# Where the high and low weight buffers of a decoder step lie in SBUF: low ones first, four small tiles between

## The chip, the cores and the metric

The kernel runs on one core of a Trainium2 chip. It is one launch. The metric is the time of the device for that launch, in microseconds, as the median over repeated runs; lower is better. One further execution is taken with the hardware profiler, and its page and trace are what is read below.

## The reference, cut to what matters

The kernel computes one layer of a hybrid decoder for 512 prompt tokens and 8 × 8 sample tokens, which share the weights (576 columns in all). Everything is float32. The places with large matrix products, which the change touches, are these:

```python
def hybrid_layer(x, mem_k, mem_v, ...):
    proj = (_rms(x) * g_pre_mix) @ w_in            # 1024 -> 5,656 columns
    z, xbc, dt_raw, q, k, v, ig, fg, og = jnp.split(proj, split_at, axis=-1)
    ...
    mix = jnp.concatenate([y_ssd, h_ml], axis=-1) @ w_out   # 2048 -> 1024
    x = x + _rms(mix) * g_post_mix
    qx = (_rms(x) * g_pre_x) @ w_xq                # 1024 -> 1024
    ...
    o = attention(qx, mem_k, mem_v) @ w_xo         # 1024 -> 1024
    x = x + _rms(o) * g_post_x
    u = _rms(x) * g_pre_ffn
    f = (jax.nn.silu(u @ w_gate) * (u @ w_up)) @ w_down     # 1024 -> 2816 -> 1024
    return x + _rms(f) * g_post_ffn, ...

mk, mv = memory_kv(mem_prompt, g_mem, w_mem_k, w_mem_v)     # two products of 256 memory rows, 1024 -> 1024
```

The convolution, the two recurrences (SSD and mLSTM, chunk by chunk) and the attention over the memory are left out here; none of them reads the buffers that move.

## The kernel before, in words

**Split products.** Activations lie with their features on the 128 partitions and their tokens along the free dimension. Each float32 operand is split in two: a high part, which is the value as the type of TensorE's fast float32 keeps it (F32R), and a low part, the rest. A product is three matmuls, summed in PSUM: high weights by high input, high weights by low input, low weights by high input. `gemm` (L195) issues such a triple for each of the 128-row blocks of the contraction, eight for an input of 1024: L202, L203 and L205. A weight tile of 128 × 1024 holds the eight 128 × 128 blocks that make 128 output features. The stationary operand of each matmul is one such block, the moving operand a run of 256, 288, 320 or 512 columns of the input. In the cross-attention output and the feed-forward the sums go by a scheme of seven products in place of eight (class `Seven`, `mul` L1846 to L1848), with the same triple over 288 columns.

**The weight buffers.** All weights come from HBM in float32 and are split on the chip. `split_w` (L172) does it for the input projection, the values, the output projection, the queries and the memory's products: SP loads into a tile `raw`, ScalarE copies it to `whi` with rounding (L180), and VectorE subtracts the two into `wlo` (L187; part of the columns on GpSimd in some tiles). Where `acc` is set, the second half of `wlo` is made in another way: ScalarE writes the negated high part (L184) and a DMA on GpSimd's queue adds the weights from HBM to it (L185). `whi` and `wlo` are each a tag with three buffers in the pool `weights`, `raw` one with two. `weights` (L1147) keeps the last three pairs by name for a second use. `cast` (L1546) and, in the feed-forward, `high1`, `parts2` and `place3` (L1794 to L1817) take buffers of the same two tags. There are other weight tiles that lie elsewhere: a second set of `whi` and `wlo` in a pool of the cross-attention, `wacc` for low parts of the feed-forward, `wmh` and `wml` for the memory's first products, `wdh` and `wdl` for the first down projections, `u3h`, `u3l` and `w3`.

**Where they lie.** A pool places a tag when its first tile is asked for, one behind the other, all buffers of a tag together. The line that asks first is L306: two pairs, `whi` then `wlo`. So the pool begins with three `whi` of 4096 bytes a partition, then three `wlo`, then the two `raw`. The pool `const` lies ahead of it.

**The small tiles.** At the end of each RMS norm over the features the reciprocal root of a token's sum of squares is made as a column. For four of these norms `root_step` (L1586) does the last Newton step on VectorE, with three short instructions, into a tile `r` of three floats a partition; `root_rows` (L1594) transposes its columns into rows on TensorE. The four tiles (`px0_r`, `p30_r`, `px1_r`, `p31_r`) are asked for in `root_step`, each with a name of its own, from the pool `const`.

**Order.** The order of the instructions on each engine is set by the scheduler at build time from a simulated timeline, under the constraints that the kernel gives with `issue_after` and, in the later stages, a plan written out as a list of positions (`at_`, L1537). Loads of weights stand on SP's queue, the adding DMAs on GpSimd's. Neither addresses nor offsets enter that order unless a buffer is shared.

Of the kernel before, what the change touches and what calls it, by code (L numbers as in the profile page):

```python
# [11 lines left out]
F32 = mybir.dt.float32  # L12
F32R = mybir.dt.float32r
# [6 lines left out]
P = 128  # L20
# [95 lines left out]
def build(nc, tc, ctx, I, O):  # L116
# [3 lines left out]
    cp = ctx.enter_context(tc.tile_pool(name="const", bufs=1))  # L120
    wp = ctx.enter_context(tc.tile_pool(name="weights", bufs=1))
# [181 lines left out]
        mm(psw[:, 0:256], wz[:, 0:128], wz, start=True, stop=True, skip_group_check=True)  # L303
    S.dma_start(par, I["par"])

    wi = [[wp.tile([P, 1024], F32R, name=k, tag=k, bufs=3) for k in ("whi", "wlo")] for _ in range(2)]  # L306
    raws = [wp.tile([P, 1024], F32, name="raw", tag="raw", bufs=2) for _ in range(2)]
    for k in range(KT):
        if k % 2 == 0:
# [24 lines left out]
    for k in range(KT):  # L334
        for (hi, lo), pss in zip(wi, ps0):
            wh, wl = hi[:, k * P:(k + 1) * P], lo[:, k * P:(k + 1) * P]
# [373 lines left out]
    for g in range(2):  # L710
# [13 lines left out]
        for h in range(8):  # L724
            k, j = h % 2, (8 * g + h) // 2
# [163 lines left out]
    for h in range(4):  # L889
        q, k = qk[:, h, :], qk[:, 4 + h, :]  # L890
# [78 lines left out]
    for hb in range(2):  # L969
        r = slice(32 * hb, 32 * hb + 32)  # L970
# [614 lines left out]

    def root_step(name):  # L1586
        v, y, a = R[name]
        r = cp.tile([P, 3], F32, name=name + "_r")
        V.tensor_tensor(a, y, y, op=ALU.mult)
        V.scalar_tensor_tensor(a, a, -0.5, v, op0=ALU.mult, op1=ALU.mult)  # L1590
        V.scalar_tensor_tensor(r, a, 1.5, y, op0=ALU.add, op1=ALU.mult)
        R[name] = r
# [11 lines left out]
    def norm(name, ssq, i, out, alloc, p, d):  # L1604

        at_(p, root_sums, name, ssq, i, alloc)
        at_(p + 0.4, root_step, name)
        at_(d, root_rows, name, i, alloc)
        at_(d + 0.2, root_copy, name, i, out)
# [744 lines left out]
```

## Time and profile before

| | |
|---|---|
| median of 3 timed runs | 1088.65 us (1088.47 to 1088.78) |
| profiled execution, its own time | 1087.01 us |
| its span | 1085.2 us |
| granted TensorE clock, mean | 0.998 |

The page gives the busy time of each engine, the span in 40 slices, the chain of work that ended last, and groups of instructions by line, engine, operation and tiles. PE is TensorE's matmuls, PEld its loading of weights, DVE is VectorE, ACT ScalarE, POOL GpSimd, and SP the engine that issues loads. A group `L205 PE MATMUL ps_in<-uh,wlo 128*128 128x256 f32 x272` has its line, its engine and operation, the PSUM tile it writes, the moving tile and the stationary one, their shapes and the count; behind the bar stand the busy time in us, the mean of one in ns, and the engine's idle time ahead of them with what ended most of it. In the matmuls in order of time each row begins with the start in us and the duration in us, rounded to 0.01.

Matmuls overlap: one takes some 300 ns from its start to its end, and starts while two others are still running. So for TensorE the distance between starts is the time that a matmul costs, and it is worked out from the first and last row of an unbroken run and the number of steps between.

### The profile page before, as it was taken

The page shows a single profiled execution, that of the slowest core. Times are in us where ns is not written, and L with a number is a line of the kernel's source. Part 1 is how long each engine was busy: PE and PEld are TensorE (multiplying, and loading weights), DVE is VectorE, ACT ScalarE, POOL GpSimd, SP SyncE. Part 2 cuts the span into 40 slices and gives each one's busy share as a digit, 9 for nine tenths or more (in the row PEclk, how much of TensorE's full clock was granted, in tenths as well). Part 3 has the DMA queues.
Part 4 walks back from the last instruction along what each step waited for, and adds up shares of the span by engine and source line. Part 5 has one row for each costly group of instructions (what it writes and reads, how often), then busy time and mean ns, then how long its engine had stood idle before and what let it go on. Part 6 is the DMA issues. An engine that isn't in the chain of part 4 may idle for free.

```text
span 1085.2 us, 20708 instructions
## 1 busy us (share of the span) xinstructions
PE 1075.0 (99%) x8124; PEld 1022.1 (94%) x8124; DVE 752.4 (69%) x1507; ACT 610.9 (56%) x1098; POOL 228.0 (21%) x305
## 2 busy tenths in 40 slices
PE   9999999999999999999999999999999999999997
PEld 9999887778999999999999989999999999999997
DVE  6896785658877775568755546766467887787556
ACT  7867632355654555656555545645566566656653
POOL 1332643313113111000154301100011111111000
PEclk9999999999999999999999999999999999999999
DMA  6775535435654449653458775643486697578532
GB/s 211 179 159 126 161 111 172 165 80 185 190 152 144 110 123 324 226 193 101 152 194 288 271 252 180 239 133 92 135 176 137 159 203 163 117 189 184 125 131 88
DMA packets 58966, 182.29 MB, mean 168 GB/s; under 512 B 6604, under 2 KB 11852, under 8 KB 58356
## 3 DMA queue, kind: packets, MB, share of 16 engines
q1 hardware_dynamic: 42740, 138.06, 38.6%
q0 software_dynamic: 15552, 41.95, 19.6%
q8 instruction: 64, 1.05, 0.4%
q10 hardware_dynamic: 576, 0.95, 0.3%
q14 instruction: 34, 0.28, 0.1%
HBM read 160.28 MB, written 20.65 MB: 167 GB/s over the span
## 4 chain that ended last, share of the span: by engine, by line
PE 86%; DVE 5%; ACT 4%; issue 2%; DMA 2%; POOL 0%; DVEq 0%; SPq 0%; ACTq 0%; POOLq 0%
PE ps_in L203 4%; PE ps_in L202 4%; PE ps_in L205 4%; PE ps_v L815 3%; PE ps_o L205 3%; PE ps_o L203 3%; PE ps_g L1846 3%; PE ps_g L1847 3%; PE ps_o L202 3%; PE ps_u L1847 3%; PE ps_u L1848 3%; PE ps_u L1846 3%; PE ps_g L1848 3%; PE ps_dn L1846 2%; PE ps_dn L1847 2%
## 5 line engine op out<-in xcount | busy, mean ns | idle before, releaser
L202 PE MATMUL ps_in<-uh,whi 128*128 128x320 f32 (+1 forms) x544 | 162.9, 300 | 0.5 <-DVE cb L451 0.5
L205 PE MATMUL ps_in<-uh,wlo 128*128 128x320 f32 (+1 forms) x544 | 162.3, 299 | 0.3 <-DMA wlo<-win 0.3
L203 PE MATMUL ps_in<-ul,whi 128*128 128x320 f32 (+1 forms) x544 | 161.8, 298 | 0.0
L180 ACT CAST whi<-raw 128x1024 fp32r<-128x1024 f32 (+1 forms) x104 | 105.2, 1013 | 100.0 <-PE ps_in L203 25.9
L187 DVE TENSOR_TENSOR wlo<-raw,whi 128x512 fp32r<-128x512 f32 (+1 forms) x96 | 93.7, 978 | 75.1 <-ACT whi L180 74.0
L202 PEld LDWEIGHTS ps_in<-uh,whi 128*128 128x128 f32 x544 | 102.8, 189 | 3.3 <-issue 1.7
L205 PEld LDWEIGHTS ps_in<-uh,wlo 128*128 128x128 f32 x544 | 102.3, 188 | 1.5 <-DMA wlo<-win 0.5
L203 PEld LDWEIGHTS ps_in<-ul,whi 128*128 128x128 f32 x544 | 102.4, 188 | 0.6
L185 POOL DMA_DIRECT2D wlo<-win x32 | 27.8, 869 | 80.7 <-ACT wlo L184 70.0
L1847 PE MATMUL ps_g<-b,whi 128*128 128x288 f32 x144 | 42.5, 295 | 0.0
L1846 PE MATMUL ps_g<-b,whi 128*128 128x288 f32 x144 | 42.4, 295 | 0.0
L1847 PE MATMUL ps_u<-b,whi 128*128 128x288 f32 x144 | 42.4, 295 | 0.0
L1846 PE MATMUL ps_u<-b,whi 128*128 128x288 f32 x144 | 42.2, 294 | 0.0
L1819 ACT CAST whi<-rawx 128x1024 fp32r<-128x1024 f32 (+1 forms) x26 | 25.6, 984 | 27.9 <-PE ps_dn L1847 13.8
L192 DVE TENSOR_TENSOR wlo<-sw,whi 128x1024 fp32r<-128x1024 f32 (+1 forms) x26 | 29.6, 1140 | 14.9 <-ACT whi L191 14.8
L202 PE MATMUL ps_xo<-qh,whi 128*128 128x288 f32 x128 | 38.5, 303 | 0.2 <-ACT whi L180 0.2
L205 PE MATMUL ps_o<-mixm_h,wlo 128*128 128x256 f32 (+1 forms) x128 | 37.9, 296 | 0.0
L1798 ACT CAST whi<-raw 128x1024 fp32r<-128x1024 f32 (+1 forms) x26 | 25.6, 983 | 21.8 <-PE ps_g L1847 9.7
L203 PE MATMUL ps_xo<-ql,whi 128*128 128x288 f32 x128 | 37.8, 296 | 0.0
L205 PE MATMUL ps_o<-mixs_h,wlo 128*128 128x320 f32 (+1 forms) x128 | 37.7, 295 | 0.0
L203 PE MATMUL ps_o<-mixs_l,whi 128*128 128x320 f32 (+1 forms) x128 | 37.7, 295 | 0.0
L203 PE MATMUL ps_o<-mixm_l,whi 128*128 128x256 f32 (+1 forms) x128 | 37.7, 295 | 0.0
(769 smaller groups left out, 3853.6 us busy)
## 6 DMA issues: line engine op xcount, KB each, us to landing
raw<-win SPq DMA_DIRECT2D x35, 512.0 KB, 4.0
raw<-wout SPq DMA_DIRECT2D x17, 512.0 KB, 3.7
raw<-wxq SPq DMA_DIRECT2D x13, 512.0 KB, 6.0
raw<-wgate SPq DMA_DIRECT2D x13, 512.0 KB, 3.6
raw<-wup SPq DMA_DIRECT2D x13, 512.0 KB, 5.1
wlo<-win POOLq DMA_DIRECT2D x24, 256.0 KB, 5.1
kva<-vc SPq DMA_DIRECT2D x11, 512.0 KB, 5.0
raw<-wv SPq DMA_DIRECT2D x10, 512.0 KB, 4.0
```

Of the source, the lines that this page charges most:

```text
L180: casts.append(A.copy(hi[:, :n], raw[:, :n]))
L185: G.dma_start(lo[:, a:b], src[:, a:b], accum_op=ALU.add)
L187: e.tensor_tensor(lo[:, a:b], raw[:, a:b], hi[:, a:b].bitcast(F32), op=ALU.subtract)
L192: (eng or V).tensor_tensor(lo, src, hi.bitcast(F32), op=ALU.subtract)
L202: mm(ps, wh, ah, start=i == 0, stop=False)
L203: mm(ps, wh, al, start=False, stop=False)
L205: m = mm(ps, tiles[order[c]][1], xh(order[c], t0, n), start=False, stop=c == len(tiles) - 1)
L815: mm(ps, a, b, skip_group_check=True, **kw)
L1798: s.c1 = A.copy(s.h1[:, s.all], s.r1[:, s.all])
L1846: mm(ps, wh, b[0][k], start=start and k == 0, stop=False, skip_group_check=True)
L1847: mm(ps, wh, b[1][k], start=False, stop=False, skip_group_check=True)
L1848: m = mm(ps, wl, b[0][k], start=False, stop=k == nk - 1, skip_group_check=True)
```

## The change

Line 306 makes the two `wlo` tiles first, then four small tiles for the roots in the same pool, then the two `whi` tiles. `root_step` takes its tile from there in place of asking the pool `const` for one.

```diff
-    wi = [[wp.tile([P, 1024], F32R, name=k, tag=k, bufs=3) for k in ("whi", "wlo")] for _ in range(2)]
+    wl = [wp.tile([P, 1024], F32R, name="wlo", tag="wlo", bufs=3) for _ in range(2)]
+    RT = {k: wp.tile([P, 3], F32, name=k + "_r", tag=k + "_r") for k in ("px0", "p30", "px1", "p31")}
+    wi = [(wp.tile([P, 1024], F32R, name="whi", tag="whi", bufs=3), lo) for lo in wl]
     raws = [wp.tile([P, 1024], F32, name="raw", tag="raw", bufs=2) for _ in range(2)]
...
     def root_step(name):
         v, y, a = R[name]
-        r = cp.tile([P, 3], F32, name=name + "_r")
+        r = RT[name]
         V.tensor_tensor(a, y, y, op=ALU.mult)
```

A tile of 12 bytes takes 32. The four tiles thus leave `const`, which ends 128 bytes earlier, and stand between the two kinds of weight buffers; from the first `raw` on, every address is what it was. In bytes from the start of a partition, as the built programs have them:

| tile | before | after |
|---|---|---|
| the four small tiles | 18016, 18048, 18080, 18112 | 30304, 30336, 30368, 30400 |
| `whi` (three buffers) | 18144, 22240, 26336 | 30432, 34528, 38624 |
| `wlo` (three buffers) | 30432, 34528, 38624 | 18016, 22112, 26208 |
| `raw` (two buffers) | 42720, 46816 | 42720, 46816 |
| `whi`, `wlo` modulo 512 | 224, 224 | 224, 96 |

Some other tiles that the prediction speaks of, before and after: `uh` begins at 69536 and `ul` at 90016 (both 160 modulo 256), `mixs_h` at 480 and `mixs_l` at 416 modulo 512; the second set of `whi` and `wlo` and `wacc` at 160 modulo 512, `wmh` at 480, `wml` at 416, `wdh` at 416, `wdl` at 160.

## The prediction

> **What bounds the kernel now.** I read the page's span, busy times and clock first, then the chain that ended last, then the matmuls grouped by shape, and last the matmuls in order of time.
>
> ```profile
> span 1085.2 us, 20708 instructions
> PE 1075.0 (99%) x8124; PEld 1022.1 (94%) x8124; DVE 752.4 (69%) x1507; ACT 610.9 (56%) x1098; POOL 228.0 (21%) x305
> PEclk9999999999999999999999999999999999999999
> PE 86%; DVE 5%; ACT 4%; issue 2%; DMA 2%; POOL 0%; DVEq 0%; SPq 0%; ACTq 0%; POOLq 0%
> ```
>
> TensorE is busy for 99% of the span at full granted clock, and the chain that ended last lies on it for 86%. Nothing else is near. A wait taken from another engine therefore buys little; what counts is the distance from the start of one matmul to the start of the next, which I call the pace. The busy time of a matmul (near 300 ns) overlaps that of its neighbours and can't be summed; the pace can. It is read from start times, in the matmuls in order of time (start, duration, engine, line, tiles, shape). Here are two runs of the same product, 256 columns, same tiles, same line:
>
> ```profile
> 157.73 0.28 PE L202 MATMUL ps_in<-uh,whi 128*128 128x256 f32 x1
> 160.35 0.28 PE L205 MATMUL ps_in<-uh,wlo 128*128 128x256 f32 x1
> ...
> 381.88 0.28 PE L202 MATMUL ps_in<-uh,whi 128*128 128x256 f32 x1
> 384.58 0.28 PE L205 MATMUL ps_in<-uh,wlo 128*128 128x256 f32 x1
> ```
>
> From first to last row are 23 steps each: 2.62/23 = 113.9 ns in the first run, 2.70/23 = 117.4 ns in the second. Neither contains a wait. So one and the same product settles into one of two paces, 3.5 to 4 ns apart, and keeps it for the whole run. Read through the same view, about half of the matmuls of this shape go at each. The products of 320 columns show a third thing:
>
> ```profile
> 384.70 0.31 PE L202 MATMUL ps_in<-uh,whi 128*128 128x320 f32 x1
> 387.78 0.31 PE L202 MATMUL ps_in<-uh,whi 128*128 128x320 f32 x1
> ...
> 398.24 0.30 PE L202 MATMUL ps_o<-mixs_h,whi 128*128 128x320 f32 x1
> 398.38 0.31 PE L203 MATMUL ps_o<-mixs_l,whi 128*128 128x320 f32 x1
> 398.53 0.31 PE L205 MATMUL ps_o<-mixs_h,wlo 128*128 128x320 f32 x1
> 398.68 0.30 PE L202 MATMUL ps_o<-mixs_h,whi 128*128 128x320 f32 x1
> ...
> 401.71 0.27 PE L202 MATMUL ps_o<-mixs_h,whi 128*128 128x256 f32 x1
> ```
>
> The input projection runs at 3.08/21 = 146.7 ns, the output projection on mixs at 3.47/24 = 144.6 ns, with unequal steps inside its triple (about 140, 145 and 150). Shape and weight buffers are the same. What differs is where the moving tiles lie: uh and ul start at the same byte modulo 256, mixs_h and mixs_l are 64 bytes apart. Places in SBUF thus go with a few per cent of the pace, and places are all that this change alters.
>
> **The change part by part.** The built program has the same instructions in the same order with the same waits on every engine, SP's and POOL's queues included. No step is moved, no wait is added, no DMA grows. Only the addresses of whi, wlo and four 12-byte tiles are new: the six weight buffers all started at 224 modulo 512; now whi starts at 224 and wlo at 96.
>
> *VectorE, ScalarE, GpSimd and the DMAs: nothing.* The rows that write whi or wlo, beside rows of the same shape whose tiles lie at differing offsets:
>
> ```profile
> L187 DVE TENSOR_TENSOR wlo<-raw,whi 128x512 fp32r<-128x512 f32 x49 | 34.8, 711 | 39.4 <-ACT whi L180 38.6
> L1820 DVE TENSOR_TENSOR u3l<-rawx,whi 128x512 fp32r<-128x512 f32 x18 | 12.4, 686 | 1.6 <-ACT whi L1819 1.6
> L184 ACT ACTIVATE wlo<-whi 128x512 fp32r<-128x512 f32 x24 | 15.0, 625 | 0.3
> L1793 ACT ACTIVATE wlo<-rawx 128x512 fp32r<-128x512 f32 x18 | 11.3, 626 | 0.0
> L205 PE MATMUL ps_in<-uh,wlo 128*128 128x256 f32 x272 | 77.3, 284 | 0.3 <-DMA wlo<-win 0.3
> wlo<-win POOLq DMA_DIRECT2D x24, 256.0 KB, 5.1
> ```
>
> L187 reads and writes three tiles at 224; L1820 reads 160 and 224 and writes 32, and is 25 ns shorter; the two ScalarE rows differ by 1 ns. Were all 95 subtractions of L187 25 ns shorter, VectorE would save 2.4 us of work; it already idles 39.4 us ahead of one form of them, waiting for ScalarE, so the cover is wide. The bounds are 0 and a gain of the 0.3 us for which TensorE waits on wlo; I take 0. The four small tiles are written by one short VectorE instruction each and read by transposes: 0, from the same reason.
>
> *TensorE.* While a product streams its moving tile, the weights of the next are being loaded. In each triple (high weights with high input, high weights with low input, low weights with high input), the step during which wlo is loaded, and the one that uses it, now meet another place. No row shows high and low weights 128 bytes apart, so I bound it by the nearest rows. Products on other weight buffers, whose low half is not at the high half's offset, are there:
>
> ```profile
> 491.86 0.28 PE L202 MATMUL ps_mk<-memhl,wmh 128*128 128x256 f32 x1
> 497.39 0.28 PE L205 MATMUL ps_mk<-memhl,wml 128*128 128x256 f32 x1
> ...
> 547.54 0.28 PE L202 MATMUL ps_mk<-memhl,whi 128*128 128x256 f32 x1
> 550.14 0.28 PE L205 MATMUL ps_mk<-memhl,wlo 128*128 128x256 f32 x1
> ...
> 1058.10 0.28 PE L203 MATMUL ps_dn<-hl,wdh 128*128 128x256 f32 x1
> 1060.71 0.28 PE L205 MATMUL ps_dn<-hh,wdl 128*128 128x256 f32 x1
> ```
>
> The same product ps_mk goes at 2.60/23 = 113.0 ns on whi and wlo (equal offsets), and at 5.53/47 = 117.7 ns on wmh and wml, which lie 64 bytes apart modulo 512: 47 steps without one return to the quick pace. ps_dn on wdh and wdl (256 apart) goes at 2.61/22 = 118.6 ns. So the quick pace of 256 columns is seen here only where high and low weights share an offset, and I take it as lost.
>
> The matmuls that use the moved buffers, from the rows grouped by shape:
>
> ```profile
> L205 PE MATMUL ps_in<-uh,wlo 128*128 128x320 f32 x272 | 85.1, 313 | 0.0
> L205 PE MATMUL ps_o<-mixm_h,wlo 128*128 128x256 f32 x64 | 18.1, 282 | 0.0
> L205 PE MATMUL ps_xq<-u2h,wlo 128*128 128x256 f32 x64 | 17.9, 279 | 0.0
> L205 PE MATMUL ps_mk<-memhl,wlo 128*128 128x256 f32 x48 | 13.6, 284 | 0.0
> L1848 PE MATMUL ps_u<-b,wlo 128*128 128x288 f32 x108 | 31.2, 295 | 0.0
> ```
>
> - 256 columns, equal input offsets: 272 + 64 + 64 + 48 = 448 triples, 1344 matmuls, half of them at the quick pace today. Losing it costs 1344 × ½ × 4.2 ns (from 113.5 to 117.7) = **+2.8 us**. Bounds: all at the quick pace, −2.8; all at 118.6, 1344 × (118.6 − 115.6) = +4.0.
> - 320 columns, equal input offsets (ps_in, and 64 triples each of ps_o and ps_xq): 400 triples, 1200 matmuls. They run at 146.7 today, have no second pace, and I take **0**. Bounds: 144.6, as mixs has it, −2.5 us; a loss in the proportion 118.6 to 117.7, 0.8%, +1.3 us.
> - mixs, and hidden tiles that are skewed likewise, in ps_o and the last down projections: some 320 matmuls of each of the two shapes. Should they lose their 2.1 ns at 320 columns, it costs 0.7 us; I take half, **+0.3**. Bounds: +0.9, and −1.4 if their 256-column part (about 118) found the quick pace.
> - 288 columns, in the cross-attention output and the feed-forward: some 1500 matmuls on moved buffers.
>
> ```profile
> 754.79 0.29 PE L1846 MATMUL ps_u<-b,whi 128*128 128x288 f32 x1
> 757.96 0.29 PE L1846 MATMUL ps_u<-b,whi 128*128 128x288 f32 x1
> ...
> 806.14 0.30 PE L1848 MATMUL ps_g<-u3h,wacc 128*128 128x288 f32 x1
> 807.47 0.30 PE L1846 MATMUL ps_g<-u3h,whi 128*128 128x288 f32 x1
> ```
>
> With whi and wlo at one offset the pace is 3.17/24 = 132.1; with wacc, 64 bytes off, 1.33/10 = 133.0. I take **0**; the bounds are ±0.9 ns × 1500 = ±1.4 us.
>
> The sum is 2.8 + 0.3 = +3.1 us, all on the path, since nothing else works on the chain inside these runs. The profiled execution took 1087.01 us, its span of 1085.2 and 1.8 around it; it would become 1090.1. The three timed runs have their median 1.64 us above it, at 1088.65, and the same step from there gives 1091.7. I say **1091.5 us**. All low bounds together give −0.3 − 2.8 − 2.5 − 1.4 − 1.4 = −8.4 us, all high ones 4.0 + 1.3 + 0.9 + 1.4 = +7.6.
>
> **The rivals.** *Faster: the offset takes a clash away.* Loading weights at a place that the streaming input isn't reading could end the longer steps. For it: mixs, where one step of three is 140 ns instead of 147. Against it: there it is the inputs that are skewed, and skewed weights (wmh, wdh) ran slow. It would have all 256-column runs at 113.5 (−2.8) and the 320-column ones at 144.6 (−2.5): −5.3, 1083.4 us. It decides once a 320-column run of ps_in paces below 146.
>
> *No change.* The two paces occur with equal places, so the pace may be set by how a run is entered, and the places of weights may not matter; then half stay quick: 1088.7 us. Against it stands the ps_mk pair. The Trainium skill says in "SBUF — State Buffer", section "Who interferes with whom", that TensorE has two independent read ports, one for the moving operand and one for loading weights, and that it waits on no one; by that rule this case is the outcome, 1088.65. The trace agrees as to ScalarE and VectorE, whose times hardly move with place, and not as to TensorE, whose triple on mixs has steps of 140 and about 150.
>
> *Slower at every width.* The stagger also costs at 320 and 288 columns, as wdh and wacc suggest: 4.0 + 1.3 + 0.9 + 1.4 = +7.6, 1096.2 us. For it: both these rows; against it: neither is 128 bytes apart.
>
> **How the numbers follow.** The forecast has 0.44, faster 0.24, no change 0.18, slower at every width 0.14. A measurement of this kernel tells about 0.2%, 2.2 us, from no change. The forecast's own spread of about 2 us reaches into that band as the no-change case reaches out of it: faster 0.24, within 0.2% 0.20, slower 0.56. The range is 1083.5 to 1097: from the faster rival's value to just above the last one's; the likeliest case's own is 1089.5 to 1094.
>
> **What would show it.** Right: 256-column runs of ps_in and ps_xq all at 117.7 or above, those of 320 columns still near 146.7, those of 288 near 132.1, with the clock, the order and the VectorE and ScalarE rows as now. Wrong: 256-column runs at 113.5 in more than half of the cases, or any shift by more than 1 ns at 320 columns, where the largest unpriced sum stands (1200 matmuls, 1.2 us for each ns); or a wait on wlo or on one of the small tiles that is not there today.

## The result and the profile after

| | before | after |
|---|---|---|
| median (18 runs each) | 1088.43 us (1087.56 to 1090.51) | 1086.45 us (1085.65 to 1088.20) |
| ratio | | 0.9983, 95% interval 0.9976 to 0.9990 |
| profiled execution, its span | 1087.01, 1085.2 us | 1087.61, 1085.8 us |

The change made the kernel faster by 0.17%, about 1.9 us by the ratio (the two medians lie 2.0 apart). That lies inside what the prediction called no change (0.2%), and clear of zero. The forecast was slower by 3 us, so it had the wrong sign. The profiled execution of after happens to be longer than that of before; why it doesn't speak against the timed runs is shown below.

The page of after, with the lines that answer to those of before:

```profile
span 1085.8 us, 20708 instructions
PE 1073.6 (99%) x8124; PEld 1020.0 (94%) x8124; DVE 752.6 (69%) x1507; ACT 611.0 (56%) x1098; POOL 226.8 (21%) x305
PEclk9999999999999999999999999999999999999998
PE 78%; DMA 6%; DVE 6%; ACT 5%; issue 3%; POOL 1%; SPq 0%; DVEq 0%; ACTq 0%; POOLq 0%
```

TensorE still works through 99% of the span. VectorE and ScalarE stand at the same busy time to 0.2 us. Of the 1.4 us that PE is less busy only part can be time gained, because busy times overlap; the paces tell more. The matmuls of after in order of time (start, duration, engine, line, tiles, shape); first the run of ps_in at 256 columns that the prediction showed at 381.88 us, and the 320-column run behind it:

```profile
382.76 0.28 PE L202 MATMUL ps_in<-uh,whi 128*128 128x256 f32 x1
...
385.48 0.30 PE L202 MATMUL ps_in<-uh,whi 128*128 128x320 f32 x1
...
388.83 0.31 PE L205 MATMUL ps_in<-uh,wlo 128*128 128x320 f32 x1
```

From the first row to the second are 24 steps, 2.72/24 = 113.3 ns, where before had 117.4. From the second to the third are 23 steps, 3.35/23 = 145.7 ns, where before had 146.7. The prediction named two clear signs of a forecast gone wrong. The first, the quick pace at 256 columns in more than half of the cases, is there in full: of the runs of ps_in of at least 21 matmuls without a break, 6 of 18 end at 113.3 ns in before (over their last nine steps), and 17 of 17 in after. The second, a shift by more than 1 ns at 320, is met at its edge: the mean step of ps_in went from 146.6 to 145.6. The products on mixs, and the memory products on the two kinds of buffers:

```profile
399.01 0.31 PE L202 MATMUL ps_o<-mixs_h,whi 128*128 128x320 f32 x1
...
402.53 0.28 PE L202 MATMUL ps_o<-mixs_h,whi 128*128 128x256 f32 x1
...
493.49 0.28 PE L202 MATMUL ps_mk<-memhl,wmh 128*128 128x256 f32 x1
...
499.14 0.28 PE L797 MATMUL ps_v<-wmh,memhl 128*128 128x256 f32 x1
...
548.83 0.28 PE L202 MATMUL ps_mk<-memhl,whi 128*128 128x256 f32 x1
...
551.43 0.28 PE L205 MATMUL ps_mk<-memhl,wlo 128*128 128x256 f32 x1
```

mixs at 320 columns lost its advantage: 3.52/24 = 146.7 ns, from 144.6. ps_mk on wmh and wml, which did not move, stays at 5.65/48 = 117.7; on whi and wlo it is at 2.60/23 = 113.0 as before, though its low weights now lie 128 bytes off.

Since both kernels issue the same 8124 matmuls in the same order, each step can be set against its counterpart. All steps that lie in unbroken runs of one width in all four traces, by width; the second profiles of both kernels were taken in the experiments:

```
columns  steps   before  before again  after  after again (mean ns)  after - before (us)
256      1970    116.65  116.60        115.82  115.87                 -1.6
288      2738    132.48  132.47        132.25  132.25                 -0.6
320      1509    146.35  146.32        145.94  145.93                 -0.6
512       256    229.99  229.99        230.36  230.39                 +0.1
outside  1650    (all other steps, us against before:) +1.6, +3.3, +1.8
```

The paces repeat between two executions to 0.05 ns; after gains 2.7 us in them. The steps outside unbroken runs vary by 1.5 us between two executions of one kernel, and the profiled execution of before was a short one (1087.01, against 1088.39 for its second profile). One part of the excess returns in both profiles of after: TensorE waits longer at two places, it seems because it comes there earlier and what it waits for does not. Two rows of before, then two of after (in brackets the idle time, and what ended it):

```profile
95.41 0.42 PE L202 MATMUL ps_in<-uh,whi 128*128 128x320 f32 x1 [0.53 <-DVE cb L451]
...
109.66 1.13 PE L616 MATMUL ps_h<-xe,btok 128*128 128x512 f32 x2 [0.29 <-POOL xe L614]
```

```profile
96.62 0.41 PE L202 MATMUL ps_in<-uh,whi 128*128 128x320 f32 x1 [0.79 <-DVE cb L453]
...
110.88 0.70 PE L618 MATMUL ps_h<-xe,btok 128*128 128x512 f32 x1 [0.46 <-POOL xe L616]
```

So 0.79 − 0.53 + 0.46 − 0.29 = 0.43 us of the gain is given back there. 2.7 − 0.4 = 2.3 us is left, and the timed runs show 1.9 (interval 1.1 to 2.6). In the second profile of after the same two waits are 0.79 and 0.44; in that of before, 0.52 and 0.29. The first profile of after has three more waits which its second lacks: 0.92 us on ssqx, 0.36 on wlo in the output projection and 0.34 on ssqm; the second has one of 0.62 on cb that the first lacks.

### The profile page after: what moved, and what is told of

Its sections match the earlier page's. It is cut to its first block, busy times and chain, and to the rows that moved or that the text cites. A ratio compares the mean times of both kernels' runs of the same rounds, so it can differ in the third digit from the quotient of the medians.

```text
span 1085.8 us, 20708 instructions
## 1 busy us (share of the span) xinstructions
PE 1073.6 (99%) x8124; PEld 1020.0 (94%) x8124; DVE 752.6 (69%) x1507; ACT 611.0 (56%) x1098; POOL 226.8 (21%) x305
## 4 chain that ended last, share of the span: by engine, by line
PE 78%; DMA 6%; DVE 6%; ACT 5%; issue 3%; POOL 1%; SPq 0%; DVEq 0%; ACTq 0%; POOLq 0%
PE ps_in L203 4%; PE ps_in L205 4%; PE ps_in L202 4%; PE ps_v L817 3%; PE ps_g L1848 3%; PE ps_u L1848 3%; PE ps_u L1850 3%; PE ps_g L1850 3%; PE ps_g L1849 3%; PE ps_u L1849 3%; PE ps_dn L1848 2%; PE ps_dn L202 2%; PE ps_dn L1849 2%; PE ps_dn L203 2%; PE ps_dn L1850 2%
## 5 line engine op out<-in xcount | busy, mean ns | idle before, releaser
L187 DVE TENSOR_TENSOR wlo<-raw,whi 128x512 fp32r<-128x512 f32 (+1 forms) x96 | 94.0, 982 | 78.3 <-ACT whi L180 77.2
L202 PE MATMUL ps_o<-mixs_h,whi 128*128 128x320 f32 (+1 forms) x128 | 37.8, 296 | 0.0
```

The source lines that it names most:

```text
L187: e.tensor_tensor(lo[:, a:b], raw[:, a:b], hi[:, a:b].bitcast(F32), op=ALU.subtract)
L202: mm(ps, wh, ah, start=i == 0, stop=False)
```

## The experiments

Three theories stood against each other. *Distance*: what counts is how far, modulo 256, the low weights lie from the high ones. *Place*: what counts is where each weight block lies against the input that streams while it is loaded. *Order*: what counts is that the buffers changed sides, or that the small tiles left the constants. I write a place as (high, low), in bytes from the inputs uh and ul modulo 256: before is (64, 64), after (64, 192).

**The order of the change without its distance.**

```diff
+    RT = {k: wp.tile([P, 3], F32, name=k + "_r", tag=k + "_r") for k in ("px0", "p30", "px1", "p31")}
     wl = [wp.tile([P, 1024], F32R, name="wlo", tag="wlo", bufs=3) for _ in range(2)]
-    RT = {k: wp.tile([P, 3], F32, name=k + "_r", tag=k + "_r") for k in ("px0", "p30", "px1", "p31")}
```

> The four small tiles first, then the low weights, then the high ones: the order of the change, but high and low weights both start at 224 modulo 512, as in the kernel before. If the distance between high and low weights decides, the gain goes: ps_in at 320 columns paces at 146.6 again (145.7 in the changed kernel), at 256 columns near 116, mixs at 320 columns back at 144.5, time near 1088.4. If it was the order of the buffers, or that the small tiles left the constants, all stays as in the changed kernel: 145.7, 114.9, mixs 146.4, near 1086.4.

Measured: 1088.76 us, ratio to before 1.0001 (0.9992 to 1.0010). ps_in at 320 columns 146.65, mixs at 320 columns 144.39, at 288 columns 132.47 (before 132.48), at 256 columns 115.97 in ps_in. A run of ps_in at 256 columns:

```profile
383.46 0.28 PE L202 MATMUL ps_in<-uh,whi 128*128 128x256 f32 x1
...
386.29 0.31 PE L202 MATMUL ps_in<-uh,whi 128*128 128x320 f32 x1
```

2.83/24 = 117.9 ns, the slow pace of before. The paces are as before the change, and so is the time. Order is out, and so are the small tiles.

**The distance with its sides exchanged: (192, 64).**

```diff
-    wl = [wp.tile([P, 1024], F32R, name="wlo", tag="wlo", bufs=3) for _ in range(2)]
+    wh = [wp.tile([P, 1024], F32R, name="whi", tag="whi", bufs=3) for _ in range(2)]
     RT = {k: wp.tile([P, 3], F32, name=k + "_r", tag=k + "_r") for k in ("px0", "p30", "px1", "p31")}
-    wi = [(wp.tile([P, 1024], F32R, name="whi", tag="whi", bufs=3), lo) for lo in wl]
+    wi = [(hi, wp.tile([P, 1024], F32R, name="wlo", tag="wlo", bufs=3)) for hi in wh]
```

> High weights first at 96 modulo 512, then the small tiles, then the low weights at 224: the distance of the change with its sides exchanged. If the distance between high and low weights decides, whichever side is moved, it behaves as the changed kernel: ps_in 145.7 at 320 columns and about 115 at 256, time near 1086.4. If the place of each weight tile relative to the streaming input decides, two of the three loads of a triple are moved here where the change moved one, and the 320-column pace moves about twice as far (144.7, some -1.9 us in place of -1 for the 320-column part), or the other way.

Measured: 1088.46 us, ratio 0.9999 (0.9990 to 1.0008). The 320-column pace of ps_in is 145.82, mixs 146.42, 288 columns 132.20: as in the changed kernel, which speaks for distance. But at 256 columns there is a pace not seen in ps_in until now:

```profile
383.46 0.28 PE L202 MATMUL ps_in<-uh,whi 128*128 128x256 f32 x1
...
386.31 0.31 PE L202 MATMUL ps_in<-uh,whi 128*128 128x320 f32 x1
```

2.85/24 = 118.8 ns, where (64, 192) has 113.3; of the 18 unbroken runs of ps_in, 12 are slow like this one and 6 are quick. So distance alone does not decide at 256 columns, and in sum over all products the paces gain only 0.3 us: −0.8 at 288, −0.2 at 320 (ps_in gains, mixs and ps_dn lose), +0.4 at 256 and +0.3 at 512 columns.

**No distance, both moved: (192, 192).**

```diff
-    wl = [wp.tile([P, 1024], F32R, name="wlo", tag="wlo", bufs=3) for _ in range(2)]
+    wh = [wp.tile([P, 1024], F32R, name="whi", tag="whi", bufs=3) for _ in range(2)]
+    wi = [(hi, wp.tile([P, 1024], F32R, name="wlo", tag="wlo", bufs=3)) for hi in wh]
     RT = {k: wp.tile([P, 3], F32, name=k + "_r", tag=k + "_r") for k in ("px0", "p30", "px1", "p31")}
-    wi = [(wp.tile([P, 1024], F32R, name="whi", tag="whi", bufs=3), lo) for lo in wl]
```

> High then low weights, both at 96 modulo 512, the small tiles behind them: no distance between high and low, both moved 128 bytes against the inputs. If the distance decides, it is the kernel before: 146.6 at 320 columns, near 116 at 256, near 1088.4. If the place against the input decides, all three loads of a triple are moved, and the pace at 320 columns moves by three times the change's 1 ns (near 143.7) or, if being unlike the neighbour is not needed, by as much as the changed kernel (145.7).

Measured: 1090.07 us, ratio 1.0013 (1.0004 to 1.0022), slower by 0.13%. At 320 columns 146.66, as before. At 256 columns no unbroken run of ps_in ends at the quick pace:

```profile
378.48 0.28 PE L202 MATMUL ps_in<-uh,whi 128*128 128x256 f32 x1
...
381.31 0.31 PE L202 MATMUL ps_in<-uh,whi 128*128 128x320 f32 x1
...
384.83 0.28 PE L202 MATMUL ps_in<-uh,whi 128*128 128x256 f32 x1
```

2.83/24 = 117.9 and 3.52/24 = 146.7 ns; over all steps of ps_in at 256 columns 117.44 (before 116.20), of ps_xq 117.82 (before 114.97). Here high and low share an offset and the quick pace is lost. So equal offsets don't bring the quick pace, on which the forecast was built; that unequal ones can have it, the changed kernel shows.

**A map of places.** Only matmuls; their loop, for each place `wm` and distance `dw` in 4-byte elements, with `dm` between the inputs:

```diff
+    for k in range(KT):
+        h = hi[:, wm + 128 * k:wm + 128 * k + 128]
+        x = (wm + dw) % 128
+        l = lo[:, x + 128 * k:x + 128 * k + 128]
+        mh = ah[:, 640 * k:640 * k + n]
+        ml = al[:, dm + 576 * k:dm + 576 * k + n]
+        TE.matmul(ps, h, mh, start=k == 0, stop=False)
+        TE.matmul(ps, h, ml, start=False, stop=False)
+        TE.matmul(ps, l, mh, start=False, stop=k == KT - 1)
```

> Only matmuls: the triple of the kernel (high weights by high input, high by low, low by high), 24 at a time at 256, 320 and 288 columns, for every combination of the place of the high weights against the input (0, 64, 128, 192 bytes), the distance of low weights from high ones (0, 32, 64, 128, 192, 256, 384), and the distance of the low input from the high one (0, 64, 128). The rest of the computation is left out. If the distance between weights decides, the rows of distance 0 and 256 or of 0 alone are the slow ones at 320 columns (146.6) for every place against the input, and 128 gives 145.6. If the place against the input decides, columns differ and rows do not. If the pace comes from how a run is entered, neighbours with equal places differ.

Measured, mean steps in ns from the fourth matmul of a run to its last, for inputs at one offset, worked out from the matmuls in order of time; rows are the place of the high weights, columns the distance of the low ones in bytes:

```
256 columns:    0     32     64    128    192    256    384
     0          -  118.3  117.8  119.5  117.8  119.7  119.5
    64      113.3  118.8  118.5  113.5  117.8  117.8  113.5
   128      118.8  117.8  116.7  118.7  117.8  118.8  118.0
   192      117.8  118.0  117.7  119.0  117.8  117.8  119.1
320 columns:    0     32     64    128    192    256    384
     0      146.7  146.7  146.8  144.7  146.2  146.6  145.7
    64      146.7  148.2  146.8  145.5  146.7  146.7  145.5
   128      146.7  146.5  144.6  146.6  146.6  146.7  144.7
   192      146.7  144.5  145.1  145.7  146.0  146.7  145.5
```

(The first run of all began at steps of 213 ns and is left out.) At 320 columns a distance of 0 or 256 gives 146.6 to 146.7 wherever the pair lies: so far distance is right. Off zero it is not the distance alone: 128 gives 144.7, 145.5, 146.6 and 145.7. Rows 0 and 128 also give two values each for distances of 128 and 384, which are equal modulo 256. At 256 columns the quick pace stands in one row, 64, and there at distances 0, 128 and 384; at 256, which is 0 modulo 256, the same place shows 117.8. At 288 columns, not shown, the row 64 has 133.3 at distance 0 and 131.1 at 128; in the kernel, whose inputs of that width lie at several offsets, 0.23 ns of that is left. So the *pair* of places decides, and at some pairs, (64, 64) among them, something more: perhaps the entry.

**The entry.** A matmul of 64 to 156 columns in steps of 4 ahead of every run of 24 (for 320 columns, in steps of 8):

```diff
+    for wm, wl in ((16, 16), (16, 48), (48, 16), (48, 48)):
+        for first in range(64, 160, step):
+            TE.matmul(banks[7][:, :first], hi[:, wm:wm + 128], ah[:, :first], start=True, stop=True)
+            ...
```

> Only matmuls, the rest is left out: before each unbroken run of 24 stands one matmul of 64 to 156 columns, so that the run is entered at 24 different distances; inputs and weights lie as in the kernel before (high 64, low 64 bytes from the inputs), as in the changed kernel (64, 192), with the sides exchanged (192, 64) and with both moved (192, 192). If the change makes the slow pace of 256 columns unstable: (64, 64) keeps 113.3 or 117.8 to its end according to the entry, some of each; (64, 192) is at 113.3 from the sixth step on for nearly all entries; (192, 192) never gets below 116. If the entry doesn't matter, all 24 runs of a place have one pace. 320 columns: one pace for a place whatever the entry, 146.6, 145.6, 145.8, 146.7 in that order.

Measured at 256 columns, over the last nine steps of each run: (64, 64) ends at 113.3 in 9 of 24 entries and at 117.8 in 14, the first of all ran at 213; (64, 192) at 113.3 in all 24; (192, 64) at 113.3 in 23, and at 118.7 in one; (192, 192) at 117.8 in all 24. At 320 columns the entry hardly matters: 146.3 to 146.9, 145.4 to 145.7, 145.3 to 145.8, 146.4 to 146.6. The change thus leaves the quick pace and makes the slow one unstable: in the map the run at (64, 192) begins with steps of 117, 119, 121, 116 and 114 ns, and goes on at 113.3.

This did not explain why (192, 64), quick in 23 of 24 entries, was slow in 12 of 18 runs in the kernel. There the runs of 256 and 320 columns follow each other, and the end of one is the entry of the next:

```diff
+    for wm, wl in PLACES:
+        for n in (320, 256) * 5:
+            ...
```

> Only matmuls, the rest is left out: unbroken runs of 24 at 320 and 256 columns in turn, as in the input projection, five times for each of twelve places. If the end of the 320-column run fixes how the 256-column run is entered, all five runs of a place have one pace, and they are those of the kernels: (64, 64) 117.8, (64, 192) 113.3, (192, 64) 118.9, (192, 192) 117.8. If the entry is a matter of chance, (64, 64) has both paces among its five and (192, 64) is mostly at 113.3, as after single matmuls of other widths.

The matmuls in order of time, from the fourth of ten runs at (64, 64), (64, 192), (192, 64) and (192, 192); the tiles ah and al stand for uh and ul:

```profile
37.93 0.28 PE L151 MATMUL ps<-ah,whi 128*128 128x256 f32 x1
...
40.76 0.31 PE L151 MATMUL ps<-ah,whi 128*128 128x320 f32 x1
...
69.51 0.28 PE L151 MATMUL ps<-ah,whi 128*128 128x256 f32 x1
...
72.23 0.30 PE L151 MATMUL ps<-ah,whi 128*128 128x320 f32 x1
...
100.72 0.28 PE L151 MATMUL ps<-ah,whi 128*128 128x256 f32 x1
...
103.57 0.31 PE L151 MATMUL ps<-ah,whi 128*128 128x320 f32 x1
...
132.52 0.28 PE L151 MATMUL ps<-ah,whi 128*128 128x256 f32 x1
...
135.34 0.31 PE L151 MATMUL ps<-ah,whi 128*128 128x320 f32 x1
```

2.83/24 = 117.9, 2.72/24 = 113.3, 2.85/24 = 118.8, 2.82/24 = 117.5 ns: those of the rows shown from the four kernels. From the third pair on, all pairs at one place have the same paces to 0.1 ns, so the entry is no matter of chance there: the 320-column run fixes it. The kernels agree where an unbroken run of just 24 at 320 columns stands directly ahead: such 256-column runs of ps_in and of ps_o on mixm are slow in 10 of 10 cases in before (9 of 10 in its second profile) and in 10 of 10 at (192, 64), and quick in 10 of 10 in after. The quick runs of before and of (192, 64) have other things ahead of them, mostly a wait, another product, or a piece of another length. In this experiment the inputs start at 128 modulo 256, in the kernel at 160, and the paces are the same: what counts is the place against the input, not the place in SBUF as such.

**All 64 pairs.**

```diff
+    for wm in range(0, 64, 8):
+        for wl in range(0, 64, 8):
+            ...
```

> Only matmuls, the rest is left out: 24 at a time at 256, 320 and 288 columns, high and low weights each at 0, 32, ... 224 bytes from the inputs, which have one place modulo 256. If the pace of 113.3 at 256 columns belongs to the high weights' place against the input, it stands in one row of eight (64) and perhaps its neighbours, whatever the low weights do; if it belongs to the distance, it stands on diagonals. For 320 columns the distance theory wants equal values along diagonals: 146.6 at 0, lower off it by up to 2.

Measured over the last 18 steps of each run, at 256 columns: only (64, 192) ran at 113.3 in this order of runs; (192, 128) came next with 115.6, and the other seven pairs 128 bytes apart ran at 117.8 to 120.2. At 320 columns all eight pairs on the main diagonal stand at 146.7 or 146.8, and the eight with 128 bytes between them at 144.4, 146.7, 145.6, 146.6, 146.7, 147.4, 145.6 and 147.8. Neither a row nor a diagonal explains it; it takes both places.

**Is it the loading of weights that gets in the way?** The four places once more, with six entries and with weight blocks of 128, 96, 64 and 32 columns:

```diff
+    for c in (128, 96, 64, 32):
+        ...
+        h = hi[:, wm + 128 * k:wm + 128 * k + c]
+        l = lo[:, wl + 128 * k:wl + 128 * k + c]
```

> Only matmuls, the rest is left out: the four places as before, six entries each, with weight blocks of 128, 96, 64 and 32 columns. If loading weights and streaming the input get in each other's way, the paces fall with the width of the block and the places stop mattering: at 32 columns all four near 113.3 at 256 columns and 320-column runs near 140, the shortest step seen so far. If the pace comes from the places of the inputs alone, 117.8 and 146.7 remain at 32 columns.

The loads grouped by shape (count, busy time in us, mean of one in ns, idle before) do get shorter:

```profile
L153 PEld LDWEIGHTS ps<-ah,whi 128*128 128x128 f32 x384 | 73.3, 191 | 0.0
L153 PEld LDWEIGHTS ps<-ah,whi 128*32 128x32 f32 x384 | 41.5, 108 | 7.6
```

At 320 columns the places agree at 32-column blocks: 146.7 over the last 15 steps in 20 of 24 runs and 145.3 to 146.6 in the others, where 128-column blocks gave 146.6, 145.5, 145.5 and 146.6 by place. At 256 columns 18 of 24 runs are at 113.3, (192, 192) with three of six among them. In between it is not a mere shrinking: with 64 columns three of the places run 320 columns at 144.4 to 144.9 on the mean, and only (64, 64) stays at 146.6. So the width of the weight block changes what a pair of places gives, and at the narrowest the pairs hardly differ at 320 columns. That speaks for the load taking part in it. It does not prove it: a narrower block also has the matmul write fewer rows of PSUM, and no run varies the one without the other. But the pace did not fall to 140, as it should if a clash with the load were all that holds 320 columns at 146.7. What holds it there stays open.

**The other side of the pair: the inputs.** 64 bytes behind mixs_h, in the pool at the upper end of SBUF, move mixs_h and what later takes its place to the offset of the other inputs; whi and wlo stay as in the changed kernel.

```diff
-    mixs_h = SL0("mixs_h")
+    mixs_h, space = SL0("mixs_h"), big0.tile([P, 16], F32, name="space", tag="space", bufs=1)
```

> The changed kernel with one more tile of 64 bytes behind mixs_h, in its pool at the upper end of SBUF: mixs_h, and the hidden, query and memory weight tiles that follow it in that place, start 64 bytes lower and are then at the same place modulo 256 as mixs_l and the other inputs. If places decide as the map has it, the 192 matmuls of mixs at 256 columns fall from 117.9 to about 113.4 (-0.85 us), those at 320 from 146.5 to 145.6 (-0.15 us), and the 256-column down projections on hidden tiles fall likewise by some 3 ns on 130 matmuls (-0.4 us): together about -1.3 us, 1085.1. If only the places of the weights count, the time is the changed kernel's.

Measured: 1085.55 us, ratio to before 0.9975 (0.9966 to 0.9984), in the same series as the changed kernel's 1086.65 below. mixs at 256 columns went from 117.90 to 113.37 and at 320 from 146.46 to 145.48; ps_dn from 118.20 to 117.11 at 256 columns and from 147.20 to 145.90 at 320. Two of its rows on mixs:

```profile
395.79 0.28 PE L202 MATMUL ps_o<-mixs_h,whi 128*128 128x256 f32 x1
...
398.51 0.30 PE L202 MATMUL ps_o<-mixs_h,whi 128*128 128x320 f32 x1
```

2.72/24 = 113.3 ns: moving the input does what moving the weights did. By its median this is the fastest version of the study. Its paces gain 1.6 us over the changed kernel, 1.1 of which reach the medians; the view of waits between 435 and 505 us shows where part of the rest went in its profiled execution (us in total, times, longest):

```profile
PE ps_o L205 <- DVE wlo L187: 1.4, 2, 0.7
```

TensorE now comes to the low weights of the output projection before VectorE has made them. In the two profiles of the changed kernel this wait was 0.4 us and none, in the first of before none.

**Both kernels again.** No edit.

> The changed kernel once more, beside the others. The paces inside unbroken runs repeat: 145.6 at 320 columns of ps_in, 132.2 at 288, ps_in at 256 near 115. What in its profile was longer than before, some 3 us outside unbroken runs of equal width (of that 2.2 us ahead of 35 us), is a matter of that one execution and goes, or halves; if it belongs to the change it returns within 0.5 us.

Measured: 1086.65 us, ratio 0.9988 (0.9979 to 0.9997), a smaller gain than at first with an interval that overlaps. Paces: 145.61, 132.25 at 288, ps_in at 256 columns 115.09. Outside unbroken runs 1.8 us more than the first profile of before; the excess of 3.3 about halved. All 18 unbroken runs of ps_in at 256 columns end at 113.3 again (7 of 18 in the second profile of before).

> The kernel before once more, for a second profile. The paces inside unbroken runs repeat to 0.05 ns at 320 and 288 columns. Its profiled execution took 1087.01 us, below the median of its timed runs, 1088.4; if the time outside unbroken runs varies from one execution to the next, a profile near the median shows 1 to 2 us more there, and the changed kernel's second profile, which had 1.8 us more there than the first of before, is no worse than before.

Measured: one execution of 1088.39 us. 146.61 and 132.47 repeat; outside unbroken runs 1.6 us more than in its first profile. Against this profile the changed kernel's two have 1.7 and 0.3 us more there; the two waits of 0.43 us in sum are the part that was found each time, the rest is not settled.

## Why the prediction failed, point by point

- *What bounds the kernel, and that only the pace of TensorE matters*: right. Instructions, order, clock and the other engines' times stayed; the steps inside unbroken runs carry the gain.
- *VectorE, ScalarE, GpSimd, DMAs: nothing*: right. The row of L187 on 512 columns of after has 710 ns where it had 711, so the 25 ns that a change of place might have taken off are not there:

```profile
L187 DVE TENSOR_TENSOR wlo<-raw,whi 128x512 fp32r<-128x512 f32 x49 | 34.7, 710 | 39.2 <-ACT whi L180 38.5
```

- *256 columns, +2.8 us*: this step failed. It had the sentence "the quick pace of 256 columns is seen here only where high and low weights share an offset, and I take it as lost". Measured: −0.87 us in ps_in, −0.48 in ps_o on mixm, −0.14 in ps_mk, −0.07 in ps_xq, −1.56 in sum. The rows shown were read rightly and the wrong variable was taken from them. ("Half of them at the quick pace today" was a little high: 6 of 18 unbroken runs of ps_in, and a mean of 116.2 where half would be 115.6.) wmh lies at 64 from its input and wml at 0; whi and wlo lay at 64 and 64. Two things differ there, distance and the low weights' own place, and (192, 192) shows that equal offsets don't bring the quick pace, (64, 192) that unequal ones have it. The pace isn't monotone in the distance either, so a row at 64 bytes bounds nothing at 128. The lower bound of −2.8, all steps at the quick pace, did hold the result.
- *320 columns at equal input offsets, 0 (bounds −2.5 and +1.3)*: wrong by 1 ns a step: ps_in −0.72, ps_o −0.20, ps_xq −0.19, −1.11 us. The prediction saw 146.7 as the only pace of this width for such inputs. In the map it is the pace of all equal places, wherever they are, and of some unequal ones, such as (64, 0); (64, 192) is not among them.
- *mixs and its like, +0.3*: right in sign and near in size, +0.38 at 320 columns and +0.03 at 256 in mixs, +0.1 in ps_dn; but half of a loss had been reckoned, and mixs lost its whole 2.1 ns. The nearness is luck.
- *288 columns, 0 (bounds ±1.4)*: −0.64 us, inside the bounds, though not nothing.
- *The rivals.* "Faster: the offset takes a clash away" has the direction, and its test (a 320-column run of ps_in below 146) came true; that a clash was taken away is not shown. Its price was too high: −5.3, where the paces gave −2.7 and two waits took 0.4 back. At 320 columns it had reckoned with 144.6 and found 145.6, and at 256 columns, where all unbroken runs of ps_in did end at the quick pace, it was −1.6 and not −2.8: (64, 192) needs some steps to leave the slow pace, which cost part of the gain (ps_in has 115.0 on the mean). "No change" is off, though its time, 1088.7, is nearer than the forecast's: ps_in at 320 columns moved in both profiles by 1.0 ns, and (192, 192) is slower beyond its interval. With it goes what the prediction drew from the rule of the Trainium skill ("SBUF — State Buffer", "Who interferes with whom"), that weight loading and the moving operand have independent ports and TensorE waits on no one. The page says nothing of places, and here they matter: alone they make 113.3, 117.8 or 118.9 ns at 256 columns. Whether the two ports get in each other's way, no run here shows. "Slower at every width" is refuted in its sign.
- *What was not priced*: that a quicker TensorE finds cb and xe not ready, 0.4 us.

What the two places do to each other inside TensorE is not shown, and the cause stays open there. What the runs show is that it isn't the distance, nor one place alone, and that it changes with the width of the weight block and with what ran before.

## What to carry to other kernels

Where TensorE is busy throughout, compare the distance between starts of one product in several runs; two paces without a wait can come from where the operands lie, and from how a run is entered. Measure a map with a kernel of matmuls alone, in the very succession of widths that the kernel uses, before pricing a shift of addresses: the nearest row of the trace may differ in two places at once, and paces do not run smoothly between rows. Move inputs as well as weights, and look at what becomes late when TensorE gains a few hundred nanoseconds.

## What the hardware showed that was not expected

With the inputs at one offset, a distance of 256 bytes gave the pace of 0 within 0.1 ns in all four rows of the map at 320 columns. An unbroken run can keep one of two paces for its whole length from its first few steps on (113.3 or 117.8 ns at (64, 64)), and an address shift of 128 bytes in one operand makes one of them unstable without changing the other. And where runs of 24 follow each other the pace is settled by the preceding run: (192, 64) is at 113.3 ns after 23 of 24 single matmuls, and at 118.8 after a run of 24 at 320 columns, in all five cases of the experiment and all ten of the kernel.
